# Inverting the scan's unit triangles as 64x64 blocks on the array's diagonal quarters, with a second set of their tiles

## The chip, the cores and the metric

The kernel runs on one core of a Trainium2 chip. Five engines work in parallel, each through its own list of instructions in a fixed order: TensorE (PE in the profile, with PEld for the loading of weights), VectorE (DVE), ScalarE (ACT), GpSimd (POOL) and SyncE (SP), which issues most DMA transfers. They wait for each other through semaphores. The metric is the time of one execution on the device in microseconds; less is better.

## The reference

The program takes 256 tokens of width 1024 through three layers. The change lies in the first one, whose mixer joins dilated window attention (8 heads) with a bidirectional RWKV-7 recurrence (8 heads of 64). Behind it come a PEER feed-forward layer and two layers of another kind. The recurrence, for each head and each of the two directions, is

```python
def wkv7_scan(r, w, k, v, kk, a, reverse):
    def step(state, inp):
        r_t, w_t, k_t, v_t, kk_t, a_t = inp
        sa = jnp.einsum('bhvk,bhk->bhv', state, -kk_t)
        state = (state * w_t[:, :, None, :]
                 + sa[..., :, None] * (kk_t * a_t)[..., None, :]
                 + v_t[..., :, None] * k_t[..., None, :])
        y = jnp.einsum('bhvk,bhk->bhv', state, r_t)
        return state, y
    _, ys = lax.scan(step, state0, xs, reverse=reverse)
```

and the two directions' outputs are added, normalised per head, scaled and gated.

## The kernel before

**Tiling.** The kernel computes the recurrence in chunks of 64 tokens. Inside a chunk the dependence of one step on the earlier ones is a unit triangular 64x64 matrix, which is inverted; between chunks a state is carried. The 8 heads are four pairs `q`, the two heads `i` of a pair on the two halves of the partitions. The 256 tokens are two tiles `t` of 128 tokens, so two chunks each (`HALVES` are the slices 0:64 and 64:128). For each pair there are four inversions, one per direction `d` and tile `t`.

**A pair's steps.** `prepare` (L606 to L679) makes decayed keys and their transposes: its TensorE work is L606, L614, L654, L659 and L670, with chains over VectorE, ScalarE and GpSimd between them (L637, for one, computes the `ar` that L659 transposes). `start(d, t)` multiplies keys with keys (L687) and masks the products to triangles (L691) in the tile PR, which holds for each head a 128x128 matrix with two 64x64 blocks on its diagonal, one per chunk, and zeros elsewhere; the zeros are written once by GpSimd (L591). `tile(d, t)` inverts the triangle by five doubling levels of two half-steps each. In the first half-step two matmuls of 128x128 (L720, one per head) multiply it with X and VectorE masks the result into PP (L721); in the second two matmuls (L725) multiply PP with X, VectorE transposes the result (L727), and a copy makes the new X (L728; `nc.any` leaves the engine to the compiler, mostly ScalarE). L735, L743 and L746 then apply the inverse; `states` (L761, L767, L768, and L595 for the outputs) carries the state over the four chunks; `finish` normalises and gates. An fp32 matmul shows as two records in the trace.

**What sets the order.** The function `weave` gets the generators of all pairs, of the attention heads, of the output projection and of some weights' work, as tasks with a list of tasks that must be done before. Going through the list while the program is built, it takes from the tasks that are free the one whose next piece can begin first by a simple cost estimate, and emits its instructions; each engine's order is then fixed. Before the change `start` of pair q, direction d, tile t waits for the inversion of the same (d, t) of pair q-1, since both use the same PR tile, and X and PP too exist once for each (d, t).

**Lines outside this stage** that the rows show: L1516 and L1523 (two small matmuls of a compressed attention in a later layer; the weights have 64 columns in the one, 64 rows and columns in the other), L1557 (score matmuls of that attention, with weights of 64 rows on either half of the rows), L345 (sums of a weight product, one column), L527, L546 and L552 (attention), L341 (VectorE's part of a weight product), L106 to L108 (weight phases).

## Time and profile before

| | us |
|---|---|
| three runs | 2334.44, 2318.8, 2332.5 |
| median | 2332.5 |
| the profiled execution | 2320.28 |
| its span, first to last instruction | 2318.2 |
| stage of the change, from the first L687 to the next weight phase | 140.3 to 402.2 |

Over the whole span TensorE is busy 2191.8 us (95%), VectorE 1735.9 (75%), ScalarE 1264.6 (55%) and GpSimd 809.6 (35%); the mean granted clock of TensorE is 0.973 of full speed. [...] In the timelines each row is a group of equal instructions one behind another: its start, its length to the end of the last (matmuls are pipelined, so the next group starts before that end), the engine, the line, the operation, output and inputs by the program's names, and the weights' rows by columns, then output partitions by columns. "g", "o" and "y" are tags of PSUM tiles.

### The profile page before, as it was taken

How to read it: one execution, taken by the hardware profiler on the slowest of the kernel's cores; microseconds unless marked ns; L12 is line 12 of the kernel's file. 1: busy time of each engine (PE TensorE's matmuls, PEld its weight loads, DVE VectorE, ACT ScalarE, POOL GpSimd, SP SyncE). 2: the span in 40 equal slices, each digit the busy share in tenths (PEclk: the TensorE clock that was granted, in tenths of full speed). 3: DMA queues.
4: the chain of work that ended last, by engine and by line, in shares of the span. 5: the costliest groups of instructions: out<-in, count | busy, mean ns of one | idle time of the engine just before them, and what ended most of it. 6: DMA issues, size and time to landing. Idle time of an engine off the chain costs nothing.

```text
span 2318.2 us, 46849 instructions
## 1 busy us (share of the span) xinstructions
PE 2191.8 (95%) x17962; PEld 2079.0 (90%) x17962; DVE 1735.9 (75%) x3278; ACT 1264.6 (55%) x2689; POOL 809.6 (35%) x811
## 2 busy tenths in 40 slices
PE   6999898789899999999999999899999999989998
PEld 3878587789799999999999999878899999979998
DVE  6888886899877888777776765678875666777664
ACT  3543532735477776555554644447556666536543
POOL 1132320569877777444444100101432221131000
PEclk8999898899999999999999999999999999989999
DMA  7422123447655666666665675323565555516663
GB/s 266 149 92 86 61 73 96 119 107 173 162 148 155 154 150 177 196 196 195 193 193 165 185 219 193 122 74 111 155 202 166 181 162 191 178 36 192 190 200 119
DMA packets 304064, 358.38 MB, mean 155 GB/s; under 512 B 24188, under 2 KB 276576, under 8 KB 302816
## 3 DMA queue, kind: packets, MB, share of 16 engines
q1 hardware_dynamic: 291456, 349.53, 50.0%
q10 hardware_dynamic: 12384, 5.86, 1.0%
q8 instruction: 141, 2.31, 0.4%
q14 instruction: 83, 0.68, 0.1%
HBM read 354.28 MB, written 1.05 MB: 153 GB/s over the span
## 4 chain that ended last, share of the span: by engine, by line
PE 76%; DVE 13%; DMA 3%; ACT 3%; issue 2%; POOL 2%; SPq 0%; ACTq 0%; DVEq 0%; POOLq 0%
PE g L106 12%; PE g L108 12%; PE g L107 12%; PE o L106 4%; PE o L107 4%; PE o L108 3%; PE g L1162 2%; PE y L1314 2%; PE o L1314 2%; PE y L1312 2%; PE o L1312 2%; PE o L1313 2%; PE y L1313 2%; DVE uT L1001 2%; DVE wl L100 2%
## 5 line engine op out<-in xcount | busy, mean ns | idle before, releaser
L99 ACT ACTIVATE wh<-raw 128x1024 fp32r<-128x1024 f32 (+3 forms) x397 | 387.1, 977 | 389.2 <-PE g L107 185.5
L100 DVE TENSOR_TENSOR wl<-raw,wh 128x1024 fp32r<-128x1024 f32 (+3 forms) x381 | 431.6, 1135 | 223.2 <-ACT wh L99 209.8
L106 PE MATMUL g<-xh,wh 128*128 128x256 f32 x1864 | 529.9, 285 | 8.7 <-ACT xh L374 5.8
L108 PE MATMUL g<-xh,wl 128*128 128x256 f32 x1864 | 525.4, 282 | 8.4 <-DVE wl L100 8.3
L107 PE MATMUL g<-xl,wh 128*128 128x256 f32 x1864 | 524.6, 282 | 4.1 <-DVE xl L375 2.7
L1001 POOL TENSOR_TENSOR ul<-uT,uh 128x512 fp32r<-128x512 f32 x320 | 411.6, 1306 | 188.4 <-ACT uh L1001 188.4
L106 PEld LDWEIGHTS g<-xh,wh 128*128 128x128 f32 x1864 | 357.5, 192 | 15.2 <-ACT xh L374 6.9
L108 PEld LDWEIGHTS g<-xh,wl 128*128 128x128 f32 x1864 | 356.2, 191 | 12.1 <-DVE wl L100 11.7
L107 PEld LDWEIGHTS g<-xl,wh 128*128 128x128 f32 x1864 | 356.4, 191 | 6.1 <-DVE xl L375 3.5
L1001 ACT ACTIVATE uh<-uT 128x512 fp32r<-128x512 f32 x384 | 221.3, 627 | 146.5 <-POOL ul L1001 76.5
L108 PE MATMUL g<-ph,ul 128*128 128x256 f32 x1024 | 291.1, 284 | 7.7 <-POOL ul L1001 7.6
L106 PE MATMUL g<-ph,uh 128*128 128x256 f32 x1024 | 292.8, 286 | 3.7 <-ACT uh L1001 2.0
L107 PE MATMUL g<-pl,uh 128*128 128x256 f32 x1024 | 289.1, 282 | 0.0
L108 PEld LDWEIGHTS g<-ph,ul 128*128 128x128 f32 x1024 | 194.7, 190 | 11.3 <-POOL ul L1001 11.1
L106 PE MATMUL o<-hh,wh 128*128 128x256 f32 x704 | 197.8, 281 | 1.6 <-DVE t L1374 1.6
L106 PEld LDWEIGHTS g<-ph,uh 128*128 128x128 f32 x1024 | 195.1, 191 | 4.6 <-ACT uh L1001 2.3
L107 PE MATMUL o<-hl,wh 128*128 128x256 f32 x704 | 197.4, 280 | 0.0
L108 PE MATMUL o<-hh,wl 128*128 128x256 f32 x704 | 197.1, 280 | 0.0
L107 PEld LDWEIGHTS g<-pl,uh 128*128 128x128 f32 x1024 | 195.3, 191 | 0.0
L1001 DVE TENSOR_TENSOR al<-G,ah 128x256 fp32r<-128x256 f32 x128 | 173.9, 1359 | 17.2
L154 POOL TENSOR_TENSOR sql<-sq,sqh 128x256 fp32r<-128x256 f32 x48 | 48.8, 1018 | 340.1 <-ACT sqh L153 336.0
L1001 DVE STREAM_TRANSPOSE uT<-u 128x1024 f32<-128x1024 f32 x128 | 157.8, 1235 | 2.3 <-DMA u<-in_peer_u_dram 1.9
(772 smaller groups left out, 5456.4 us busy)
## 6 DMA issues: line engine op xcount, KB each, us to landing
u<-in_peer_u_dram SPq DMA_DIRECT2D x512, 128.0 KB, 2.6
raw<-in_ffn_w_gate_dram SPq DMA_DIRECT2D x44, 1024.0 KB, 5.6
raw<-in_ffn_w_up_dram SPq DMA_DIRECT2D x44, 1024.0 KB, 5.3
u<-in_peer_v_dram SPq DMA_DIRECT2D x64, 512.0 KB, 4.3
uT<-in_peer_v_dram SPq DMA_DIRECT2D x64, 512.0 KB, 4.2
raw<-in_ffn_w_down_dram SPq DMA_DIRECT2D x32, 1024.0 KB, 5.1
raw<-in_ada_w_dram SPq DMA_DIRECT2D x24, 1024.0 KB, 5.2
raw<-in_w_in_dram SPq DMA_DIRECT2D x13, 1024.0 KB, 5.7
```

The source lines that it names most:

```text
L99: nc.scalar.activation(h, v, AF.Copy)
L100: self.sub.tensor_tensor(l, v, h.bitcast(F), op=OP.subtract)
L106: nc.tensor.matmul(out, sh, mh, start=first, stop=False)
L107: nc.tensor.matmul(out, sh, ml, start=False, stop=False)
L108: nc.tensor.matmul(out, sl, mh, start=False, stop=last)
L154: self.sub.tensor_tensor(l, sq, h.bitcast(F), op=OP.subtract)
L1001: return lambda *args, **kw: self.tc.keep_in_program_order(f(*args, **kw))
L1162: nc.tensor.matmul(p[:, t], g[:, t], b[:, t], start=True, stop=True)
L1312: nc.tensor.matmul(o, vh[:, s], ah, start=i == 0 and c % 2 == 0, stop=False, skip_group_check=True)
L1313: nc.tensor.matmul(o, vh[:, s], al, start=False, stop=False, skip_group_check=True)
L1314: nc.tensor.matmul(o, vl[:, s], ah, start=False, stop=i == NB - 1, skip_group_check=True)
```

## The change

Every 128x128 block-diagonal matrix of the inversion becomes two 64x64 blocks that lie one above the other, chunk 0 on partitions 0 to 63 and chunk 1 on 64 to 127, so X, PP and the new tile PA (the triangle and the key product that L735 uses) are half as wide. A half-step is four matmuls of 64x64 (head `i`, chunk `r`), each on the quarter of the array that its partitions give, all into one PSUM tile. The masks and the identity are 64 wide. What the outputs still need as a full block-diagonal matrix stays in PR; the finished inverse is copied into a block-diagonal tile TT by two copies, whose zeros GpSimd writes once. PR, PA, X, PP, TT and `sn` get a name that ends in q % 2, so two sets exist. In the list for `weave`, `start` of (q, d, t) now waits for the inversion of (q-2, d, t) instead of (q-1, d, t), and `finish` of q waits for `finish` of q-1.

```diff
@@ -447,23 +447,32 @@
     nc.vector.tensor_tensor(xi, pi, fi, op=OP.bitwise_xor)
     xf = pool.tile([128, 128], F, name="xf")
     nc.vector.tensor_copy(xf, xi)
-    up = pool.tile([128, 128], F, name="up")
-    nc.vector.tensor_tensor(up, pi, fi, op=OP.is_lt)
-    lo = pool.tile([128, 128], F, name="lo")
-    nc.vector.tensor_tensor(lo, pi, fi, op=OP.is_gt)
-    m = keep.tile([128, 2, 8, 128], F, name="masks")
-    t = pool.tile([128, 128], F, name="mt")
+    k.bm = keep.tile([128, 128], F, name="bm")
+    nc.vector.tensor_scalar(k.bm, xf, 64.0, None, op0=OP.is_lt)
+
+    pc = pool.tile([128, 64], I32, name="pc")
+    nc.vector.tensor_scalar(pc, pi[:, 0:64], 63, None, op0=OP.bitwise_and)
+    fc = fi[:, 0:64]
+    xi, xf = xi[:, 0:64], xf[:, 0:64]
+    nc.vector.tensor_tensor(xi, pc, fc, op=OP.bitwise_xor)
+    nc.vector.tensor_copy(xf, xi)
+    up = pool.tile([128, 64], F, name="up")
+    nc.vector.tensor_tensor(up, pc, fc, op=OP.is_lt)
+    lo = pool.tile([128, 64], F, name="lo")
+    nc.vector.tensor_tensor(lo, pc, fc, op=OP.is_gt)
+    m = keep.tile([128, 2, 8, 64], F, name="masks")
+    k.unit = keep.tile([128, 64], F, name="unit")
+    nc.vector.tensor_tensor(k.unit, pc, fc, op=OP.is_equal)
+    t = pool.tile([128, 64], F, name="mt")
     for d, tri in enumerate((up, lo)):
-        nc.vector.scalar_tensor_tensor(m[:, d, 6], xf, 64.0, tri, op0=OP.is_lt, op1=OP.mult)
-        nc.vector.tensor_tensor(m[:, d, 7], m[:, d, 6], k.ident, op=OP.add)
+        nc.vector.tensor_copy(m[:, d, 6], tri)
+        nc.vector.tensor_tensor(m[:, d, 7], tri, k.unit, op=OP.add)
         for i in range(6):
             b = float(1 << i)
             nc.vector.scalar_tensor_tensor(t, xf, b, tri, op0=OP.is_ge, op1=OP.mult)
             nc.vector.scalar_tensor_tensor(m[:, d, i], xf, 2 * b, t, op0=OP.is_lt, op1=OP.mult)
-            nc.vector.tensor_tensor(m[:, d, i], m[:, d, i], k.ident, op=OP.add)
+            nc.vector.tensor_tensor(m[:, d, i], m[:, d, i], k.unit, op=OP.add)
     k.masks = m
-    k.bm = keep.tile([128, 128], F, name="bm")
-    nc.vector.tensor_scalar(k.bm, xf, 64.0, None, op0=OP.is_lt)
 
 
 def selectors(k, pool):
@@ -671,14 +680,16 @@
         self.bon = self.t1("bon")
         nc.vector.tensor_mul(self.bon, self.vT, p)
         self.yp = None
-        self.W, self.PB = [None] * 2, [[None] * 2 for _ in range(2)]
+        self.W, self.PB, self.PA = [None] * 2, [[None] * 2 for _ in range(2)], [[None] * 2 for _ in range(2)]
 
     def start(self, d, t):
 
         k, nc, pool = self.k, self.k.nc, self.late
         up = k.masks[:, d]
         az, btk = self.az[d][:, t].rearrange("p i a t -> p (i a) t"), self.btk[d]
-        PR = self.blocks(pool, f"PR{d}{t}", [128, 2, 2, 2, 128])
+
+        self.PA[d][t] = PA = pool.tile([128, 2, 2, 64], F, name=f"PA{d}{t}{self.q % 2}")
+        PR = self.blocks(pool, f"PR{d}{t}{self.q % 2}", [128, 2, 2, 128])
         self.PB[d][t] = pool.tile([128, 2, 128], F, name=f"PB{d}{t}{self.q % 2}")
         ps = [k.pw([128, 2, 2, 64]) for _ in range(2)]
         for x in range(2):
@@ -687,10 +698,11 @@
                 nc.tensor.matmul(ps[x][r].rearrange("p i a t -> p (i a) t"), btk[:, x, n], az[:, :, r], start=True, stop=True)
         yield
         for x in range(2):
+            nc.vector.tensor_tensor(PA[:, x], ps[x][:, :, 0], up[:, 6, None].to_broadcast([128, 2, 64]), op=OP.mult)
+        for x in range(2):
             for r in HALVES:
-                nc.vector.tensor_tensor(PR[r, :, x, :, r], ps[x][r], up[r, None, 6:8, r].to_broadcast([64, 2, 2, 64]),
-                                        op=OP.mult)
-        nc.gpsimd.tensor_copy(self.PB[d][t], PR[:, :, 0, 1])
+                nc.vector.tensor_tensor(PR[r, x, :, r], ps[x][r, :, 1], up[r, 7, None].to_broadcast([64, 2, 64]), op=OP.mult)
+        nc.gpsimd.tensor_copy(self.PB[d][t], PR[:, 0])
 
     def tile(self, d, t):
 
@@ -699,40 +711,43 @@
             self.yp = k.psum([128, T], tag="y", bufs=2)
         m = k.masks
         up, lo = m[:, d], m[:, 1 - d]
-        bc = lambda x: x[:, None, :].to_broadcast([128, 2, 128])
-        PR = k.zeroed[f"PR{d}{t}"]
-        X = pool.tile([128, 2, 2, 128], F, name=f"X{d}{t}")
-        pp = pool.tile([128, 2, 128], F, name=f"PP{d}{t}")
-        MA = PR[:, :, 0, 0]
-
-        nc.gpsimd.tensor_tensor(MA, MA, bc(k.ident), op=OP.add)
+        bc = lambda x: x[:, None, :].to_broadcast([128, 2, 64])
+        PR, PA = k.zeroed[f"PR{d}{t}{self.q % 2}"], self.PA[d][t]
+        X = pool.tile([128, 2, 2, 64], F, name=f"X{d}{t}{self.q % 2}")
+        pp = pool.tile([128, 2, 64], F, name=f"PP{d}{t}{self.q % 2}")
+        tt = self.blocks(pool, f"TT{d}{t}{self.q % 2}", [128, 2, 128])
+        MA = PA[:, 0]
+
+        ic = [(i, r) for i in range(2) for r in HALVES]
+
+        nc.gpsimd.tensor_tensor(MA, MA, bc(k.unit), op=OP.add)
         nc.gpsimd.tensor_tensor(X[:, 0], MA, bc(up[:, 0]), op=OP.mult)
         yield
 
         nc.vector.transpose(X[:, 1], X[:, 0])
         for i in range(2):
             r = slice(64 * i, 64 * i + 64)
-            self.ymm(i, self.yp[r, t * 128:(t + 1) * 128], self.vn[:, t, r], PR[:, i, 1, 1])
+            self.ymm(i, self.yp[r, t * 128:(t + 1) * 128], self.vn[:, t, r], PR[:, 1, i])
         for lv in range(1, 6):
             yield
-            p = k.pw([128, 2, 128])
-            for i in range(2):
-                nc.tensor.matmul(p[:, i], MA[:, i], X[:, 1, i], start=True, stop=True)
+            p = k.pw([128, 2, 64])
+            for i, r in ic:
+                nc.tensor.matmul(p[r, i], MA[r, i], X[r, 1, i], start=True, stop=True)
             nc.vector.tensor_mul(pp, p, bc(lo[:, lv]))
             yield
-            p = k.pw([128, 2, 128])
-            for i in range(2):
-                nc.tensor.matmul(p[:, i], pp[:, i], X[:, 0, i], start=True, stop=True)
+            p = k.pw([128, 2, 64])
+            for i, r in ic:
+                nc.tensor.matmul(p[r, i], pp[r, i], X[r, 0, i], start=True, stop=True)
             if lv < 5:
                 nc.vector.transpose(X[:, 1], p)
-            nc.any.tensor_copy(X[:, 0], p)
+                nc.any.tensor_copy(X[:, 0], p)
+        for r in HALVES:
+            nc.any.tensor_copy(tt[r, :, r], p[r])
         yield
-        tt = X[:, 0]
-        z0 = pp.rearrange("p i t -> p (i t)")[:, 0:128]
+        z0 = pp.rearrange("p i t -> p (i t)")
         p = k.pw([128, 128])
-        for i in range(2):
-            s = slice(64 * i, 64 * i + 64)
-            nc.tensor.matmul(p[:, s], PR[:, i, 1, 0], self.vn[:, t, s], start=True, stop=True)
+        for i, r in ic:
+            nc.tensor.matmul(p[r, HALVES[i]], PA[r, 1, i], self.vn[r, t, HALVES[i]], start=True, stop=True)
         nc.any.tensor_copy(z0, p)
         yield
         if self.W[d] is None:
@@ -766,7 +781,7 @@
                     p = k.pw([128, 128])
                     nc.tensor.matmul(p, nbk[r, 1, t], self.vn[r, t], start=True, stop=False)
                     nc.tensor.matmul(p, nbk[r, 0, t], u[r], start=False, stop=True)
-                    sn = pool.tile([128, 128], F, name="sn", bufs=6)
+                    sn = pool.tile([128, 128], F, name=f"sn{self.q % 2}", bufs=6)
                     if step:
                         st = pool.tile([128, 128], F, name="st", bufs=2)
                         nc.vector.tensor_add(st, cur[d], p)
@@ -940,10 +955,10 @@
                     first.append((("pre", q), pairs[q].prepare(), tuple(("s", q - 1, d, t) for d in range(2) for t in range(2))
                                   + ((("fin", q - 2),) if q > 1 else ())))
                 first.append((("st", q), pairs[q].states(), tuple((q, d, t) for d in range(2) for t in range(2))))
-                first.append((("fin", q), pairs[q].finish(mix[1][:, q]), (("st", q),)))
+                first.append((("fin", q), pairs[q].finish(mix[1][:, q]), (("st", q),) + ((("fin", q - 1),) if q else ())))
                 for d, t in ((0, 0), (1, 1), (0, 1), (1, 0)):
                     first.append((("s", q, d, t), pairs[q].start(d, t), ((("pre", q),) if q else ())
-                                  + (((q - 1, d, t),) if q else ())))
+                                  + (((q - 2, d, t),) if q > 1 else ())))
                     last.append(((q, d, t), pairs[q].tile(d, t), (("s", q, d, t),)))
             heads = [(("att", h), dilated_attention(k, pt, qk[0], qk[1], vn, mix[0], h), (("att", h - 1),) if h else ())
                      for h in range(8)]
```

In the changed kernel's own numbering the level matmuls are L735 and L740, their VectorE partners L736 and L742 (with the copy L743), the copies into TT L745, the former L735 is L750, `start`'s matmuls L698 and its masks L701 and L704; lines of the second half of the program move by 15.

Each engine's order before and after, at two places. The first is TensorE's list around the `prepare` of pair 1. Names: X00 and PP00 are the tiles of direction 0 and tile 0; az and btk are `start`'s inputs, with the direction behind them; the numbers behind the underscore tell instances apart; "x2" is two matmuls. Before, the starts of pair 1 stand one by one, each behind the last step (L746) of the same tile of pair 0:

```order
L743 MATMUL o128_2003<-PP00_1636,X00_1635 128x64 x2
L725 MATMUL g127_1997<-X11_1639,PP11_1640 128x128 x2
L746 MATMUL o128_2003<-X00_1635,na00_1172 64x128 x2
L687 MATMUL g129_2010<-az0_1122,btk0_1710 64x256 x2
L687 MATMUL g130_2011<-az0_1122,btk0_1710 64x256 x2
L527 MATMUL o131_2017<-qk11_378,qk01_374 128x256 x2
L735 MATMUL g132_2027<-vn0_1063,PR11_1590 128x64 x2
L720 MATMUL g133_2031<-X01_1653,PR01_1600 128x128 x2
```

After the change, with a name's third digit for q % 2, the four starts of pair 1 (inputs btk0_1724 and btk1_1832) stand together right behind the last matmul of its `prepare` (L679), while pair 0's inversions (X000, X110) are still in hand:

```order
L679 MATMUL g102_1916<-kd01_1709,bm_245 128x256
L698 MATMUL o103_1924<-az0_1128,btk0_1724 64x256 x2
L698 MATMUL g104_1925<-az0_1128,btk0_1724 64x256 x2
L345 MATMUL g105_1930<-one_69,acc_1580 128x1 x4
L698 MATMUL g106_1940<-az1_1271,btk1_1832 64x256 x2
L698 MATMUL o107_1941<-az1_1271,btk1_1832 64x256 x2
L698 MATMUL g108_1965<-az0_1128,btk0_1724 64x256 x2
L698 MATMUL g109_1966<-az0_1128,btk0_1724 64x256 x2
L698 MATMUL o110_1982<-az1_1271,btk1_1832 64x256 x2
L698 MATMUL g111_1983<-az1_1271,btk1_1832 64x256 x2
L604 MATMUL y116_2031<-PR001_1921,vn1_1686 64x128 x2
L735 MATMUL g112_1998<-X000_1656,PA000_1587 64x64 x4
```

So the eight groups of L698 moved ahead of pair 0's levels, and pair 1's tiles may begin any time after them.

The second place is TensorE's list while `states` of pair 0 runs (L767, L768 and L595 before; L782 and L783 after) among the inversions of pair 1. L767 and L768 take weights of 64 rows by 128 columns, L720, L725 and L595 here 128 by 128. Before:

```order
L720 MATMUL g168_2253<-X00_2073,PR00_1581 128x128 x2
L725 MATMUL o169_2257<-X11_2077,PP11_2078 128x128 x2
L767 MATMUL g170_2262<-vn0_1063,nbk10_1306 128x128
L768 MATMUL g170_2262<-W10_2041,nbk10_1306 128x128
L720 MATMUL g171_2269<-X01_2132,PR01_1600 128x128 x2
L720 MATMUL o172_2274<-X10_2192,PR10_1620 128x128 x2
L595 MATMUL y75_1634<-ar00_1119,sn_2216 128x64
L725 MATMUL g173_2278<-X00_2073,PP00_2074 128x128 x2
```

After:

```order
L735 MATMUL o157_2345<-X001_2032,PA001_1920 64x64 x4
L740 MATMUL g158_2351<-X111_2038,PP111_2039 64x64 x4
L735 MATMUL g159_2358<-X011_2044,PA011_1961 64x64 x4
L782 MATMUL o160_2368<-vn0_1069,nbk10_1312 128x128
L783 MATMUL o160_2368<-W10_2243,nbk10_1312 128x128
L740 MATMUL g161_2373<-X001_2032,PP001_2033 64x64 x4
L735 MATMUL g162_2380<-X111_2038,PA111_1936 64x64 x4
L555 MATMUL o163_2386<-ident_61,sc_2221 128x128 x4
L740 MATMUL g164_2392<-X011_2044,PP011_2045 64x64 x4
```

Here the inversions of pair 1 (names that end in 1) are groups of 64x64 weights, and between them stand weights of 64 by 128 (L782, L783) and of 128 by 128 (L555).

## Rows read from the trace of the kernel before

**Rows 1.** The head of the page.
```profile
span 2318.2 us, 46849 instructions
```

**Rows 2.** Windows A to F: stretch, length, busy (instructions), granted clock, DMA share, GB/s.
```profile
core 0: us, PE busy (x) PEld busy (x) DVE busy (x) ACT busy (x) POOL busy (x), PEclk, DMA share, GB/s
140.30:169.50 29.20, 25.23 (x163) 18.65 (x163) 27.41 (x72) 13.98 (x35) 15.29 (x21) 0.88 0.07 25
169.50:233.90 64.40, 64.36 (x495) 53.98 (x494) 54.75 (x139) 22.23 (x64) 16.73 (x18) 1.00 0.26 83
233.90:257.60 23.70, 19.58 (x104) 13.89 (x102) 19.08 (x50) 13.74 (x34) 6.41 (x5) 0.78 0.14 46
257.60:279.00 21.40, 18.46 (x133) 12.33 (x134) 20.11 (x51) 5.91 (x14) 12.23 (x14) 1.00 0.18 51
279.00:303.40 24.40, 18.81 (x132) 16.07 (x131) 22.73 (x61) 15.67 (x38) 5.77 (x5) 0.93 0.12 42
303.40:389.80 86.40, 85.46 (x668) 73.59 (x666) 70.79 (x172) 29.06 (x72) 7.77 (x14) 1.00 0.33 105
389.80:402.20 12.40, 6.51 (x26) 4.02 (x26) 4.59 (x11) 2.04 (x5) 0.00 (x0) 0.50 0.20 60
```

**Rows 3.** Waits of TensorE in the stage: total us, times, longest.
```profile
PE o L659 <- DVE ar L637: 6.6, 4, 3.8
```

**Rows 4.** Timeline of TensorE: levels, with two groups of `states` between them; L735.
```profile
187.88 0.56 PE L735 MATMUL o<-vn,PR 128*128 128x64 f32 x4
188.27 1.00 PE L345 MATMUL g<-one,acc 128*128 128x1 f32 x8
...
211.98 0.61 PE L725 MATMUL g<-X,PP 128*128 128x128 f32 x4
212.52 0.49 PE L767 MATMUL g<-vn,nbk 64*128 64x128 f32 x2
212.84 0.38 PE L768 MATMUL g<-W,nbk 64*128 64x128 f32 x2
213.16 0.71 PE L720 MATMUL o<-X,PR 128*128 128x128 f32 x4
213.70 0.61 PE L720 MATMUL g<-X,PR 128*128 128x128 f32 x4
214.15 0.61 PE L725 MATMUL g<-X,PP 128*128 128x128 f32 x4
```

**Rows 5.** Timeline of TensorE: weights of 64 rows or 64 columns, here and later.
```profile
141.62 0.60 PE L687 MATMUL o<-az,btk 128*64 128x256 f32 x4
142.06 0.60 PE L687 MATMUL g<-az,btk 128*64 128x256 f32 x4
...
1497.98 2.05 PE L1516 MATMUL g<-ce,w 128*64 128x30 f32 x32
...
1501.76 0.29 PE L1523 MATMUL o<-cg,w 64*64 64x15 f32 x4
1501.98 0.60 PE L119 MATMUL o<-one,R 1*128 1x1 f32 x4
...
1526.36 0.59 PE L1557 MATMUL g<-kd,qT 64*128 64x256 f32 x2
1526.80 0.27 PE L1556 MATMUL g<-kd,qT 64*128 64x128 f32 x1
...
1527.02 0.38 PE L1557 MATMUL g<-kd,qT 64*128 64x256 f32 x1
1527.13 0.38 PE L1557 MATMUL o<-kd,qT 64*128 64x256 f32 x1
```

**Rows 6.** Groups by form, stage: line, operation, count, busy us, mean ns, idle before.
```profile
L721 DVE TENSOR_TENSOR PP<-g,masks 128x256 f32<-128x256 f32 x52 | 21.2, 413 | 4.2 <-PE g L720 3.5
L727 DVE STREAM_TRANSPOSE X<-g 128x256 f32<-128x256 f32 x41 | 17.4, 433 | 3.3 <-PE g L725 3.2
L763 DVE TENSOR_TENSOR W<-W,g 64x128 f32<-64x128 f32 x15 | 4.2, 283 | 3.4 <-PE g L761 3.1
L591 POOL MEMSET PR<- 128x1024 f32 x3 | 2.8, 947 | 0.0
```

## Prediction

> **What bounds the kernel now.** I read the page's head first: the span is 2318.2 us [rows 1], and the time of that execution is 2320.28 us, 2.1 us more. Everything that the change edits runs in one stage, from the first L687 matmul (140.3 us) to the start of the next weight phase (402.2 us). So I read the windows of that stage next, cut where pair 1's, 2's and 3's `prepare` begin or end on TensorE: A (start of pair 0 and prepare of 1), B (tiles of 0 and 1), C (prepare 2), D, E (prepare 3), F (tiles 2 and 3, to the end) [rows 2]. The reader is to see two kinds of stretch. In B, TensorE is busy 64.36 of 64.40 us, and in the first part of F 85.46 of 86.40, at a granted clock of 1.00: there TensorE alone is the bound. In A, C and E it is busy 25.23 of 29.20, 19.58 of 23.70 and 18.81 of 24.40, while VectorE is busy 27.41, 19.08 and 22.73: there TensorE waits for the chains of `prepare`. The waits say for what: L659, a transpose of `prepare`, waited 6.6 us in four waits for `ar` of VectorE [rows 3]. So an inversion that costs TensorE less is worth its whole saving in B and F, and only a part in A, C and E.

> **TensorE, per instruction.** A half-step of a level (L720 or L725) is two fp32 matmuls of 128x128 weights, which the trace shows as four records. From one such group to the next go 0.45 us (213.70 to 214.15), and 0.39 for L735 (187.88 to 188.27) [rows 4]. There are 160 half-steps (2 directions, 2 tiles, 4 pairs, 5 levels, 2 halves) and 16 L735.

> After the change each is four matmuls of 64x64 weights, eight records. No row of before shows such a group, so I bound it. Records on 64x64 weights occur only at L1523: four, with 15 columns each, take 0.22 us to the next line, a change of weights' shape included [rows 5]. Thirty-two records with 64 columns of weights and 30 moving columns (L1516), one after another, take 2.05 [rows 5], which is 0.064 each, or 0.058 without the drain of the last (about 0.2); so eight in turn would take 0.46 to 0.51. Records on the two row halves of the array do overlap where they alternate: L1557 with 256 moving columns starts 0.11 us apart when its weights stand in the other half than the record before (1527.02 to 1527.13), against 0.44/2 = 0.22 a record when two follow each other in one half (1526.36 to 1526.80) [rows 5]. The new code alternates halves, so eight records should cost four turns, 4 x 0.058 to 4 x 0.064 = 0.23 to 0.26; I take 0.24. The bounds are 0.22 (what L1523's four took) and 0.51.

> [...]

> **Changes of shape.** Where weights of another shape follow, TensorE loses time: from 211.98 to 213.70 are 1.72 us for twelve records with two such changes (128 rows to 64, and back) [rows 4]; twelve at 0.45/4 are 1.35, so a change costs 0.185. I take 0.18 (0.17 to 0.195). Counted along the instruction order of the stage there are 184 such changes before and 283 after, because 64x64 groups now stand between work of 128x128, 128x64 and 64x128. The second piece of the order, shown with the change, is an example: two changes in its eight rows before (into L767 and out of L768), four in its nine rows after (L782, L783, and into and out of L555).

> The sum on TensorE: 160 x (0.45 - 0.24) = 33.6 off, 16 x (0.39 - 0.24) = 2.4 off, 99 x 0.18 = 17.8 on. Net **18.2 us less**. Half of what the smaller blocks save goes into changes of shape.

> **Where it falls.** Groups of levels and L735 together, counted in each stretch of the order, are 17, 68, 3, 8, 22, 58 before in A to F, and 14, 67, 7, 34, 10, 44 after. The changes are 13, 52, 22, 15, 8, 74 and 23, 74, 17, 55, 29, 85. The second set of tiles moves the starts of a pair to just behind its prepare (first piece of the order), so that its levels come earlier: those of pair 2 in D, out of E and F. With these prices, and the other work that changes place (starts, states, attention), TensorE's work changes by about -3, -10, -6, +21, 0, -19 (sum -17.5, within the rounding of 18.2).

> What of it reaches the time? B and F: TensorE has no gap there, but the turn of one tile gets longer than its share of the engine. A half-step's way is 0.24 on TensorE, 0.27 until the last record has drained (0.61 less three starts of 0.11 [rows 4]), 0.28 on VectorE (L763 [rows 6]) and two hand-overs, which no row prices and which I bound by 0.05 and 0.4: together 0.85 to 1.2 us by that estimate; four tiles at 0.24 and their changes fill that barely. Along the new order seven or eight pairs of steps stand closer than that. I charge B 1.8 and F 0.6, hence -8.5 and -18. In C only prepare's own chain is left, so of -6 I count -1; of A's -3, where that chain holds a part, -2; E, -1. In D 21.40 us held 18.46 of TensorE work: of +21 some 3 fall into its gaps, +17.5. The sum is -2 - 8.5 - 1 + 17.5 - 1 - 18 = **-13 us**.

> **VectorE, ScalarE, GpSimd.** L721 took 413 ns on 128x256, L727 433 [rows 6]; at half width they should be near the 283 of L763 (64x128) [rows 6]. 80 x 0.13 plus 80 x 0.14 is 21 us less of VectorE. It is charged at nothing: in B VectorE is busy 54.75 of 64.40, not the bound [rows 2], and with some 70 operations 0.135 shorter it would need 45 to TensorE's 54. The masks of L691, 64 operations, become 96 of half the elements each: charged at nothing, at worst 96 x 0.28 less 64 x 0.28, 9 us, which the 21 cover. The last X now goes to TT by two copies of half the size instead of one: 16 tiles, some 0.3 us later each (one more operation like L763), hidden while three other tiles are in hand. POOL gets 16 memsets instead of 4 (947 ns for 128x1024) [rows 6], in bytes 1.5 times as much, so about 2 us more; it is busy 6.41 of 23.70 in C and so has room. Its two operations at the head of each tile are halved. Weight loads, DMA and `states` are untouched; behind the stage the order of the engines is the same but for one load's place.

> The profiled execution goes from 2320.3 to 2307. The median of before is 12.2 us above that execution, so on the scale of the median: 2332.5 - 13 = **2319**.

> **The rivals.**
> R1, slower: the two halves take turns, by the PSUM tile that they share. The place is each of the 176 groups, the price 0.45 instead of 0.24: +37 on -18.2, so +18.8 (the longer groups cover each other's way, so nothing for stalls): 2351; at 0.50, 2360. The change turns from gain to loss at 0.24 + 13/176 = 0.31. For it: no row shows halves in one tile overlapping. Against: L687's column halves write different partitions of one tile (four records of 256 columns in 0.44, from 141.62 to 142.06) [rows 5], so two may write one tile at once there.
> R2, no gain: each half-step is bound by its way and not by TensorE. If the estimate of 0.85 to 1.2 us is short by 0.08 us for each of the 160 half-steps, 13 us are lost: 2332. For it: B's four tiles alone give the cover. Against: the order has `states`, attention and weights' work in between.
> R3, more gain: A, C and E shrink with VectorE's load, since prepare's operations wait behind half-width ones. Then of TensorE's gaps there, 4.0 + 4.1 + 5.6 us [rows 2], most close: A 24, C 17, E 21 instead of 27, 22.5, 23.4, 11 more, and without the 2.4 of B and F: 2306. For it: VectorE was idle only 2 to 5 us in each. Against: the waits are for long chains over three engines [rows 3].
> [...]

> **How the numbers follow.** The forecast (2312 to 2327 by the bounds of group and change without the turns) has 0.43, R3 0.22, R2 0.17, R1 0.10, R4 0.04; 0.04 remains for a gain beyond R3 (the group at 0.22 and changes at 0.17 too, below 2297). About 1%, 23 us, is what a measurement of this kernel can tell from no change: below 2309 is faster, above 2356 slower. Faster: R3 but for its upper end, and the remainder, 0.25. Slower: R4 and the half of R1 with groups near 0.50, 0.09. Same: 0.66. The range 2297 to 2344 leaves out R1, R4 and the remainder, 0.18.

> **What would show it.** Eight records of the half-steps (L735 and L740 in the changed kernel's own numbering) in 0.22 to 0.26 us would confirm the price; 0.45 or more is R1. The shape changes show as gaps of 0.15 to 0.2 between starts. B should last about 56 us and D 39; C and E about as long as now (R3: 17 and 21). [...] I am wrong most easily in the price of a 64x64 group, which no row shows, and in how the gaps of `prepare` behave when pairs overlap.

## The result, and the profile after

| | median us | lowest to highest | runs |
|---|---|---|---|
| before | 2328.13 | 2316.53 to 2334.44 | 15 |
| changed | 2347.68 | 2334.37 to 2358.59 | 15 |

The changed kernel is slower: its time is 1.0079 of the time before (95% interval 1.0062 to 1.0096), about 19 us, where 13 us less were forecast. Its profiled execution took 2349.32 us, near its median; that of before (2320.28) lies 8 us under the median of its 15 runs, so of the 29 us between the two profiles about 10 are chance. Of the 29 us, 24 lie in the stage, the rest ahead of it and behind it. How far two executions of one stage can lie apart shows the old code with trial stretches behind it (below): in the stage TensorE has the same instructions in the same order, and to the same place, the start of L797, it took 263.7 us instead of 254.1. The two rows, of the kernel before and of that run, have the columns of [rows 2]:

```profile
140.30:394.41 254.11, 235.93 (x1703) 191.24 (x1702) 215.30 (x541) 101.37 (x256) 64.20 (x77) 0.95 0.23 75
140.20:403.88 263.68, 249.11 (x1709) 200.56 (x1707) 215.94 (x543) 101.74 (x256) 63.23 (x78) 0.89 0.23 73
```

TensorE waited less there (14.6 us idle against 18.2), but its clock was lower and its work took 13 us longer.

The windows of the changed kernel, cut at the same places of the program as those of before (A to F, F in two pieces), answer [rows 2]. Columns: stretch, length, busy time (instructions) of the five engines, granted clock, DMA share, GB/s.

```profile
core 0: us, PE busy (x) PEld busy (x) DVE busy (x) ACT busy (x) POOL busy (x), PEclk, DMA share, GB/s
142.70:172.05 29.35, 21.43 (x201) 13.64 (x200) 24.44 (x74) 13.11 (x32) 15.42 (x32) 0.83 0.06 24
172.05:237.08 65.03, 61.27 (x757) 46.67 (x756) 45.36 (x143) 19.96 (x70) 10.51 (x16) 0.84 0.20 66
237.08:261.20 24.12, 15.53 (x104) 10.94 (x104) 19.08 (x50) 14.53 (x35) 5.74 (x5) 0.68 0.26 88
261.20:315.39 54.19, 51.83 (x446) 37.64 (x445) 35.00 (x106) 12.98 (x39) 10.90 (x16) 0.66 0.19 59
315.39:346.00 30.61, 26.95 (x159) 17.65 (x157) 18.47 (x50) 13.50 (x37) 6.05 (x5) 0.61 0.07 19
346.00:416.00 70.00, 68.06 (x724) 54.22 (x724) 53.38 (x155) 20.81 (x54) 5.03 (x12) 0.96 0.33 105
416.00:428.70 12.70, 6.81 (x28) 4.25 (x28) 4.85 (x12) 2.04 (x5) 0.20 (x2) 0.51 0.25 68
```

The stage lasts 286.0 us instead of 261.9. The column to read is the granted clock (PEclk), TensorE's as a share of full speed. Before, it was 1.00 in B, D and the first part of F; now it is 0.84 in B, 0.66 in D and 0.61 in E. Of 54 slices of 1 us of D (261.2 to 315.2) 50 read 0.50 or 1.00, and in the other four, at 0.54 to 0.84, it changes between these two; so a mean of 0.66 says that TensorE spent 68% of D at the lower level, 0.50. Summed over these rows that is 125 us at the lower level, where [rows 2] give 33. (Here and below "low time" is twice the missing share of the clock, times the length. By the mean clock of the whole stage, by which the runs below are compared, it is 126 against 31.)

TensorE's timeline shows what a group costs at either level: the 64x64 groups at 197 us at full clock, those at 205 us at the lower one. Columns as in [rows 4].

```profile
196.87 0.40 PE L735 MATMUL g<-X,PA 64*64 64x64 f32 x8
197.10 0.40 PE L740 MATMUL g<-X,PP 64*64 64x64 f32 x8
197.34 0.40 PE L750 MATMUL o<-vn,PA 64*64 64x64 f32 x8
...
203.57 0.79 PE L782 MATMUL g<-vn,nbk 64*128 64x128 f32 x2
204.16 0.63 PE L783 MATMUL g<-W,nbk 64*128 64x128 f32 x2
204.72 0.69 PE L735 MATMUL o<-X,PA 64*64 64x64 f32 x8
205.20 0.64 PE L740 MATMUL g<-X,PP 64*64 64x64 f32 x8
205.63 0.64 PE L735 MATMUL g<-X,PA 64*64 64x64 f32 x8
```

At full clock a group goes to the next in 0.23 to 0.24 us: the forecast's price, about half of the 0.45 of [rows 4]. At the lower level it takes 0.43 (205.20 to 205.63), so 45% of the time spent there is lost. Eight records in 0.23 us, where eight in turn would take 0.46 or more by the forecast's bound, also mean that the two row halves do overlap in one PSUM tile.

TensorE's waits in the stage (total, times, longest) answer [rows 3], and VectorE's groups [rows 6].

```profile
PE g L668 <- DVE ar L646: 10.0, 3, 4.7
PE y L604 <- DVE PR L704: 3.0, 2, 1.6
PE o L740 <- DVE PP L736: 2.8, 2, 2.5
PE g L740 <- DVE PP L736: 2.0, 3, 1.2
```

```profile
L736 DVE TENSOR_TENSOR PP<-g,masks 128x128 f32<-128x128 f32 x49 | 13.6, 282 | 9.4 <-PE g L735 8.5
L742 DVE STREAM_TRANSPOSE X<-g 128x128 f32<-128x128 f32 x43 | 13.0, 307 | 6.8 <-PE g L740 6.1
```

The half-width VectorE operations take 282 and 307 ns, near the forecast 283. But each engine now waits for the other: L736 waited 8.5 us for L735 where L721 waited 3.5 for L720 (the rows with tag g), and TensorE waits for L736, for the masks (L704) and longer for `prepare` (10.0 us for `ar`, 6.6 before). TensorE is idle 286.0 - 251.9 = 34.1 us of the stage, before 261.9 - 238.4 = 23.5.

### The profile page after: what moved, and what is told of

Same layout as the page of the kernel before. It is cut to its first block, busy times and chain, and to the rows that moved or that the text cites. A ratio compares the mean times of both kernels' runs of the same rounds, so it can differ in the third digit from the quotient of the medians.

```text
span 2347.6 us, 48300 instructions
## 1 busy us (share of the span) xinstructions
PE 2210.6 (94%) x18666; PEld 2074.2 (88%) x18666; DVE 1714.8 (73%) x3319; ACT 1258.7 (54%) x2700; POOL 799.4 (34%) x823
## 4 chain that ended last, share of the span: by engine, by line
PE 74%; DVE 14%; DMA 4%; issue 3%; ACT 3%; POOL 2%; SPq 0%; DVEq 0%; ACTq 0%; POOLq 0%
PE g L106 11%; PE g L108 11%; PE g L107 11%; PE o L106 3%; PE o L107 3%; PE o L108 3%; PE g L1177 2%; PE o L1328 2%; PE y L1328 2%; PE o L1329 2%; PE y L1329 2%; PE y L1327 2%; PE o L1327 2%; DVE uT L1016 2%; DVE wl L100 2%
```

## The experiments

The question was why the clock fell. Theory A1: waits of TensorE bring it down, and the shorter groups made more of them. A2: the 64x64 groups do so themselves, waits or not. B: it is the order with two pairs in hand (two sets of tiles). Each kernel's row of the windows over its whole stage, from the first `start` matmul to the next weight phase, stands in its own part; the columns are those above. Ratios are to the kernel before on the same chip, whose median was 2327.8, 2327.9 and 2328.7 in the three groups of runs; ratio and interval are taken over all runs, so they need not be the quotient of the medians.

**The disputed thing by itself.** Behind the stage of the kernel before stand five trial stretches, each after some 13 us of full 128x128 matmuls (`small` is the four 64x64 matmuls of a half-step, halves in turn; `full` the two 128x128 ones).

```diff
+    for _ in range(150):
+        small(p, B[0])
...
+    for _ in range(45):
+        small(p, B[0])
+        keep(nc.tensor.matmul(w[:, 0, 0:64], e, B[0][:, 0], start=True, stop=True))
...
+    for _ in range(35):
+        full(p, C[0])
+        keep(nc.tensor.matmul(w[:, 0], e[0:64], C[0][0:64, 0], start=True, stop=True))
...
+    for _ in range(35):
+        p = k.psum([128, 2, 64])
+        small(p, B[1])
+        keep(nc.vector.tensor_copy(B[1], p))
...
+    for _ in range(30):
+        p = k.psum([128, 2, 128])
+        full(p, C[1])
+        keep(nc.vector.tensor_copy(C[1], p))
```

> The kernel before with five trial stretches behind the stage, each after 13 us of 128x128 matmuls: (1) 150 groups of four 64x64 matmuls with nothing between them, (2) the same groups, each followed by one matmul of 128x128 weights, so with changes of shape, (3) 128x128 groups alternating with matmuls of 64x128, changes of shape on full blocks, (4) 64x64 groups that each wait for a VectorE copy of the last, (5) 128x128 groups that wait in the same way. Waits alone (A1): 1 to 3 at a clock of 1.00, 4 and 5 fall to 0.50. Blocks alone (A2): 1, 2 and 4 fall, 3 stays, 5 may stay. Changes of shape: 2 and 3 fall, 1 stays. The time is that of before plus about 230 us and says nothing.

The windows of the five, the last two cut where the clock changes, and the timeline of TensorE at these two cuts:

```profile
425.62:460.76 35.14, 35.14 (x1201) 35.07 (x1201) 0.00 (x0) 0.00 (x0) 0.00 (x0) 1.00 0.02 5
473.91:507.26 33.35, 33.35 (x451) 27.33 (x451) 0.00 (x0) 0.00 (x0) 0.00 (x0) 1.00 0.01 2
520.27:557.15 36.88, 36.88 (x212) 28.44 (x210) 0.00 (x0) 0.00 (x0) 0.00 (x0) 1.00 0.00 1
570.30:576.19 5.89, 3.13 (x58) 2.18 (x57) 2.04 (x7) 0.00 (x0) 0.00 (x0) 0.99 0.01 3
576.19:606.15 29.96, 19.34 (x224) 14.15 (x224) 7.88 (x27) 0.00 (x0) 0.00 (x0) 0.50 0.00 1
621.19:627.23 6.04, 3.45 (x22) 2.50 (x20) 2.12 (x5) 0.00 (x0) 0.00 (x0) 1.00 0.00 0
627.23:669.87 42.64, 30.25 (x101) 23.16 (x101) 10.20 (x24) 0.00 (x0) 0.00 (x0) 0.50 0.00 0
```

```profile
575.35 0.45 PE L825 MATMUL g<-bn,ident 64*64 64x64 f32 x8 [0.39 <-DVE bn L849]
576.19 0.69 PE L825 MATMUL g<-bn,ident 64*64 64x64 f32 x8 [0.39 <-DVE bn L849]
577.27 0.69 PE L825 MATMUL g<-bn,ident 64*64 64x64 f32 x8 [0.39 <-DVE bn L849]
578.36 0.69 PE L825 MATMUL g<-bn,ident 64*64 64x64 f32 x8 [0.39 <-DVE bn L849]
...
626.00 0.71 PE L829 MATMUL g<-bc,ident 128*128 128x128 f32 x4 [0.52 <-DVE bc L854]
627.23 1.22 PE L829 MATMUL g<-bc,ident 128*128 128x128 f32 x4 [0.52 <-DVE bc L854]
628.97 1.22 PE L829 MATMUL g<-bc,ident 128*128 128x128 f32 x4 [0.52 <-DVE bc L854]
```

The first three stretches, without a wait, stay at 1.00: 64x64 groups alone (35.14/150 = 0.234 each), the same with changes of shape, and full blocks with changes of shape. The last two, where each group waits for VectorE (0.39 and 0.52 us a time), fall to 0.50 some 6 us after they begin and stay there, whatever the block. So in these stretches waits of a fraction of a microsecond, repeated after every group, bring the clock down by themselves; neither the small block nor the change of shape does. They make up 0.39 of 0.84 us there, far more than in the kernel, where TensorE is idle for 34 of 286 us: the stretches show that waits suffice, not yet that they did it in the kernel. A step of the fourth stretch takes 0.84 us at full clock (575.35 to 576.19) and 1.09 at the lower one (577.27 to 578.36): where TensorE waits anyway, 23% is lost and not 45% (in the fifth 1.23 and 1.74, so 29%). One alternating pair of the second stretch takes 33.35/45 = 0.74; less 0.234 for the group and 0.195 for two records on full weights (half of the 0.39 of L735, [rows 4]), its two changes of shape cost 0.31, an estimate of 0.155 each.

**The blocks alone**: 64x64, but one set of tiles (all six names lose their q % 2) and the old order of starts and `finish`.

```diff
-        X = pool.tile([128, 2, 2, 64], F, name=f"X{d}{t}{self.q % 2}")
+        X = pool.tile([128, 2, 2, 64], F, name=f"X{d}{t}")
...
-                                  + (((q - 2, d, t),) if q > 1 else ())))
+                                  + (((q - 1, d, t),) if q else ())))
```

> The 64x64 blocks with one set of their tiles: names without q % 2, starts wait for the inversion of the pair before again. In the changed kernel TensorE's granted clock stood at its lower level for about 130 us of the stage and its end, before for 48. Theory A (the 64x64 groups bring the clock down): the low time stays above 100 us and the kernel at 2340 to 2350. Theory B (the order with two pairs in hand does, by the waits and changes of shape it makes): low time near 50 us again, 2310 to 2320, faster than before.

```profile
142.00:414.20 272.20, 244.98 (x2413) 179.50 (x2412) 199.43 (x587) 98.20 (x271) 50.99 (x81) 0.82 0.22 70
```

2337.98 us, ratio 1.0030 (1.0004 to 1.0056). The low time is 98 us. The blocks alone bring most of it (theory B falls as the sole cause), but by the medians they explain only half of the loss. (The profiled execution, 2345.77, is one of the slow ones of its ten; the table below has the low time of all.)

**The second set alone**: 128x128 blocks as before, with a second PR, X and PP for two of the four (direction, tile); there is no room in the on-chip memory for all four (the tiles would need 87.25 kB in each partition where 80.16 are left).

```diff
+    def two(self, d, t):
+        return self.q % 2 if d == t else 0
...
-        X = pool.tile([128, 2, 2, 128], F, name=f"X{d}{t}")
+        X = pool.tile([128, 2, 2, 128], F, name=f"X{d}{t}{self.two(d, t)}")
...
-                                  + (((q - 1, d, t),) if q else ())))
+                                  + (((q - 2 + (d != t), d, t),) if q > 1 - (d != t) else ())))
```

> The 128x128 blocks of before, with a second set of PR, X and PP for two of the four (direction, tile), (0,0) and (1,1), whose starts then wait for the pair before the last; there is no room for all four. If the short groups' waits are the cause, full groups with more pairs in hand leave TensorE no more idle than before: low time in the stage 25 to 45 us, time 2320 to 2334. If the order of two pairs itself is the cause (starts in a heap, masks of two pairs on VectorE), waits on the masks and a low time above 60 us, 2338 or more.

```profile
140.50:413.50 273.00, 245.99 (x1708) 195.07 (x1707) 221.87 (x551) 102.48 (x259) 63.10 (x79) 0.92 0.22 70
```

2338.05 us, ratio 1.0036 (1.0014 to 1.0059): the low time (44 us) is what A1 expected, the time what B did. So two of the four second sets cost some 10 us with full blocks too (3 to 14 by the interval). The stage is 11 us longer than before. Idle time grew by 3.5 us (27.0 against 23.5) and low time by 12, at 23 to 45% of itself 3 to 5 us; the rest isn't accounted for, and the profile of before, 8 us under its median, is part of it. With 64x64 blocks it costs the same: 2347.7 against 2338.0. I had not forecast a cost of this part at all.

**Each half-step twice**: the same four matmuls again, into the same place. They were left out of the cost estimate that `weave` uses, yet in the trace TensorE's order still differs from the changed kernel's. So `weave` alone does not fix the order, as the description of the kernel put it; what else does is not shown.

```diff
             for i, r in ic:
                 nc.tensor.matmul(p[r, i], MA[r, i], X[r, 1, i], start=True, stop=True)
+            for i, r in ic:
+                extra(nc.tensor.matmul(p[r, i], MA[r, i], X[r, 1, i], start=True, stop=True))
...
             for i, r in ic:
                 nc.tensor.matmul(p[r, i], pp[r, i], X[r, 0, i], start=True, stop=True)
+            for i, r in ic:
+                extra(nc.tensor.matmul(p[r, i], pp[r, i], X[r, 0, i], start=True, stop=True))
```

> The changed kernel with each half-step's four 64x64 matmuls issued twice into the same place (the result is the same; the order of the instructions differs too, as it is made from estimates). A group then lasts 0.47 us, as long as the 0.45 of before. Theory A1 (the clock falls because shorter groups leave TensorE waiting): the waits are filled, low time back to 50 to 60 us, and the kernel at 2340 to 2352 (the saving of 36 us is given back, the 99 changes of shape at 0.18 remain). Theory A2 (64x64 groups keep the clock low, waits or not): low time 130 us or more, and the doubled groups add 37 us or more: 2385 or above.

```profile
140.10:418.10 278.00, 250.96 (x3692) 198.85 (x3691) 209.52 (x604) 93.74 (x254) 52.86 (x88) 0.91 0.22 69
```

2342.70 us, ratio 1.0060 (1.0034 to 1.0086): 1280 more records on TensorE (37 us of work), and by the medians the kernel is 5 us faster than the changed one (the two intervals overlap, so it is safe to say only that it is no slower). The low time is 50 us. A2 would have had 2385 or more; it falls.

**Only the first half-step twice** (the first of the two additions above).

> As the run with every half-step issued twice, but only the first half-step of each level is doubled: TensorE's work is 18 us less than there (80 groups at 0.235). If the waits decide the clock, the low time lies between that run's (50 us in the stage) and the changed kernel's (126). If it stays near 60, the kernel comes to 2325 to 2332, no slower than before; if it goes back above 100, the gain is given away again and it stays at 2340 to 2350.

```profile
140.20:416.80 276.60, 246.93 (x3052) 188.81 (x3051) 205.49 (x594) 95.69 (x264) 55.10 (x88) 0.86 0.22 70
```

2333.97 us, ratio 1.0040 (1.0019 to 1.0060), low time 77 us: between the two, as A1 has it; a little above the 2325 to 2332 of its better branch.

**Idle matmuls in `prepare`**, ten per direction, on values that come ready while TensorE waits for `ar`; in the kernel before and in the changed one. Their results are unused.

```diff
+    def fill(self, x, n=2):
+        p = self.k.psum([128, T])
+        for _ in range(n):
+            extra(self.k.nc.tensor.matmul(p, x[:, 0:128], x, start=True, stop=True))
...
             self.kd.append(kd)
+            self.q and self.fill(kd)
...
             nc.scalar.activation(ep, L, AF.Exp)
+            self.q and self.fill(ep)
```

> The kernel before, with idle matmuls in prepare of pairs 1 to 3: ten of 128x256 for each direction, on values that come ready one after another while TensorE waits for ar (about 4.3 us of TensorE each time, 26 in all, results unused). If waits bring the clock down, the low time of the stage falls from 31 us to under 15, which gives back about 8; the idle matmuls cost what they exceed the 13 us of waits, 5 to 15. So 2320 to 2337. If waits don't matter, the low time stays at about 30 and the time is 2338 to 2350.

> The changed kernel with the same idle matmuls in prepare. If the low clock begins at the waits of prepare, the low time of the stage falls from 126 us to 60 to 90, worth 18 to 33 us, less 5 to 15 that the idle matmuls exceed the waits by: 2325 to 2342. If the short waits inside the inversion decide it, the low time stays above 100 and the time is 2350 to 2370.

First the kernel before with them, then the changed one:

```profile
140.20:428.60 288.40, 264.56 (x1829) 214.48 (x1828) 227.06 (x559) 101.38 (x251) 61.17 (x77) 0.96 0.21 66
```

```profile
141.60:429.10 287.50, 256.70 (x2533) 195.68 (x2532) 203.85 (x593) 95.50 (x265) 54.21 (x88) 0.88 0.21 67
```

2353.17 us (1.0116, 1.0082 to 1.0151) and 2354.63 us (1.0111, 1.0069 to 1.0153). As a remedy both failed, and my sums for them were 12 to 16 us too low: the idle matmuls fill few waits. What they tell is the clock: in the changed kernel the low time fell from 126 to 69 us though no half-step was touched. That it begins at the waits of `prepare` is not shown by this, for TensorE's idle time fell by only 3 us (34.1 to 30.8); the added 128x256 matmuls may do it as dense work. In the kernel before it fell from 31 to 23, not under 15, and that is less than the old code varies by itself (25 and 58 us in its two rows shown with the result).

**One set of tiles, with the first half-step, or both, issued twice.**

> 64x64 blocks with one set of tiles, and the first half-step of each level issued twice. If the two parts add up as they did so far (the second set cost the 64x64 kernel 10 us, 2348 against 2338; doubling the first half-step gave back 14, 2348 to 2334), this is 2324 (2318 to 2331), level with the kernel before or just under it, with a low time of 40 to 75 us in the stage. If instead the low clock in the one-set kernel has another cause than short groups, doubling only adds its 18 us of work: 2345 to 2356.

> 64x64 blocks with one set of tiles, and both half-steps issued twice, so that a group is as long as before (0.47 against 0.45). What then remains of the change is VectorE's shorter work (21 us, charged at nothing) and some 110 more changes of shape, at 0.155 to 0.19 us: 17 to 21 us more on TensorE. If short groups bring the clock down: a low time in the stage of 25 to 45 us as before, and 2333 to 2348 from the changes of shape alone. If the low time stays near 98, the blocks themselves and not their shortness do it.

```profile
140.50:408.90 268.40, 244.10 (x3052) 186.13 (x3051) 202.65 (x592) 96.37 (x266) 50.95 (x80) 0.87 0.22 72
```

```profile
141.40:415.70 274.30, 252.97 (x3693) 199.02 (x3692) 204.84 (x597) 96.27 (x261) 49.59 (x80) 0.91 0.22 71
```

The first came to 2323.96 us, ratio 0.9977 (0.9960 to 0.9994), low time 70 us: the sum of the parts (2324) to the microsecond, which is luck in part, as the interval leaves 4 us to either side. It is the only kernel here that is faster than before, by 4.7 us. (Its profiled execution, 2329.42, is its slowest run; its windows are to be read with that.) The second came to 2334.24, ratio 1.0027 (1.0010 to 1.0044), as expected from the changes of shape; its low time, 49 us, is a little above the 25 to 45. With doubled half-steps the second set costs 10.0 us (2333.97 against 2323.96) and 8.5 us (2342.70 against 2334.24), as it did without.

**All kernels side by side.** Every run's mean clock over the whole program is on record too, so the low time can be had for all runs and not for the profiled one alone. It includes the rest of the program, where nothing changed.

| | idle of TensorE in the stage, us | low time in the stage, us | low time of the whole run, median, us | runs |
|---|---|---|---|---|
| before | 23.5 | 31 | 140 | 58 |
| changed | 34.1 | 126 | 216 | 15 |
| one set | 27.2 | 98 | 198 | 10 |
| full blocks, second set | 27.0 | 44 | 138 | 8 |
| first half-step twice | 29.7 | 77 | 159 | 10 |
| both twice | 27.0 | 50 | 126 | 9 |
| one set, first half-step twice | 24.3 | 70 | 144 | 12 |
| one set, both twice | 21.3 | 49 | 135 | 12 |
| before, idle matmuls | 23.8 | 23 | 120 | 4 |
| changed, idle matmuls | 30.8 | 69 | 169 | 4 |

The clock goes with the time where no instruction differs: over the 15 runs of the changed kernel (182 to 236 us of low time) a straight line rises by 0.37 us for each us of low time, over the 58 of before (111 to 168) by 0.21. Making both half-steps longer again takes the low time back to that of before (126 and 135 against 140), with the same 64x64 blocks: it was the shortness of the groups that lowered the clock. But TensorE's idle time does not put the kernels in order: at 27 us of it the low time in the stage is 98, 44 and 50. So the link between short groups and the low clock is not the sum of the waits that the trace shows, and which of them, or what beside them, makes it is open.

## Why the prediction was wrong

**The prices were right.** A 64x64 group at full clock takes 0.234, forecast 0.24. R1 is out: groups that take turns would need 0.46 or more, and the trace gives half of that; two matmuls on diagonal quarters that write different partitions of one tile overlap. A half-step's way was put at 0.85 to 1.2 us with hand-overs that no row priced; a step of the fourth trial stretch, whose group also waits for VectorE and VectorE for it, took 0.84 at full clock. There are 283 changes of shape, as counted, and by the second trial stretch one costs some 0.155, forecast 0.18. VectorE's half-width operations are nearly as short as assumed.

**The step that failed is "What of it reaches the time?".** It charged each wait with its own length, 5 us in all, put the clock at nothing in the sum, and left a fall of it over all of B, R4, a chance of 0.04. [Rows 2] held the warning: in every stretch where TensorE waited (A, C, E and the stage's end) the clock was below 1.00, and where it did not (B and F's first part) at 1.00; only D, idle for 2.9 us, kept 1.00. I read the low clock as part of `prepare`, not as something that other stretches could get, although I had written that four tiles of shorter groups "fill that barely". Together they were a reason to give the clock more than 0.04. What the profile shows instead: in the stage TensorE's busy time is 13.5 us longer (251.9 against 238.4) where the sum had 18.2 less, and its idle time 10.6 longer where 5 were charged. Of the 37 us between forecast and profiled stage some 32 are slower work and 5 the waits themselves.

The clock accounts for this by stretches, within wide bounds. Low time costs 23% (where TensorE waits) to 45% (where it doesn't) of itself; in A, C, E and F I count only the low time beyond that of [rows 2]. Taken off what was measured:

| | low time counted | measured | less the clock's cost | forecast |
|---|---|---|---|---|
| A | 3 | 29.4 | 28.0 to 28.7 | 27.2 |
| B | 21 | 65.0 | 55.6 to 60.2 | 56 |
| C | 5 | 24.1 | 21.9 to 23.0 | 22.5 |
| D | 37 | 54.2 | 37.6 to 45.7 | 39 |
| E | 20 | 30.6 | 21.4 to 25.9 | 23.4 |
| F | 6 | 82.7 | 80.0 to 81.3 | 80.8 |

Each forecast lies in or within a microsecond of its bounds, which are up to 8 us wide. The stage was forecast 13 us shorter and is 24 us longer; the 92 us of added low time cost 21 to 41, and that difference is 37. By the medians of all runs the added low time is 76 us; at 0.21 to 0.37 of itself that is an estimate of 16 to 28 us out of the 33 between forecast and measurement. So the clock is most of the miss or half of it, not surely all.

**The rivals.** R4 named the mechanism, the clock at its lower level where short groups leave TensorE waiting, but put it in B alone and as all or nothing, for 54 us; it came as low time in D, B and E, for 21 to 41. R2 named the place (a half-step's way), which may be part of what starts it: TensorE waited 4.8 us for L736. But all of its idle time grew by 10.6 us, where R2 needed 13 beside the 5 I had charged, and waits of that length alone would not have reached 2348. R3 is out: A and C are no shorter, E is longer.

**The second set** was costed at nothing beyond its changes of shape. Undoing it is worth 8.5 to 10 us in three pairs of kernels by the medians (8 to 15 by the ratios), and adding it to full blocks costs 10 too. Much of it is waiting: TensorE's idle time in the stage is 5 to 7 us longer with the second set in the three pairs and 3.5 in the fourth, while the low time of the whole run is 15 to 18 us longer in two of the four and no longer in the others. Which wait it is, is not settled: TensorE waits for the masks of the starts that now stand together (3.0 us for L704), but no run took that wait away.

**What stays open** is also by what the short groups lowered the clock: idle matmuls in `prepare` removed 57 us of low time, longer half-steps 49 to 76, and these overlap; in none of these did idle time fall by more than some 7 us.

## What to carry to other kernels

Before work is taken off an engine that is the bound, ask what will fill its place: on TensorE the clock can fall (in D from 1.00 to 0.66), and at the lower level, 0.50, a 64x64 group takes 0.43 us, nearly the 0.45 of the full block at full clock, so the whole saving is gone there. Read the granted clock of every stretch beside the waits, and of every run beside its time: stretches with waits and a clock below 1.00 (here A, C and E, 0.78 to 0.93) next to gapless ones at 1.00 (B) are the sign that there is something to lose. And of a change in two parts, test each alone: here the part meant to give cover (the second set) cost 10 us with either block size, while the smaller blocks were worth 5 us once the first half-steps were made longer again (with both made longer they cost 6).

## What was not expected of the hardware

```profile
286.00:293.00 7.00, 6.54 (x74) 4.84 (x72) 3.00 (x11) 2.24 (x8) 2.50 (x2) 0.96 0.47 150
294.00:317.00 23.00, 23.00 (x172) 15.89 (x168) 12.21 (x32) 7.24 (x20) 0.00 (x0) 0.50 0.18 55
```

For 23 us the records show no gap, and the clock remained at 0.50; in the 7 us ahead of the fall TensorE had stood still for only 0.46 us. The kernel with one set of tiles shows the same in B: 0.34 us of waiting in 10.24, then 13.7 us without a gap at the lower level.

```profile
187.73:197.97 10.24, 9.90 (x117) 7.30 (x114) 7.30 (x23) 4.33 (x15) 6.77 (x11) 1.00 0.29 90
197.97:211.63 13.66, 13.66 (x91) 9.04 (x90) 8.70 (x28) 1.46 (x5) 2.38 (x5) 0.50 0.13 38
```

Between the fourth and the fifth trial stretch, by contrast, full 128x128 matmuls brought the clock back while they ran:

```profile
606.15:610.00 3.85, 3.85 (x11) 3.13 (x10) 0.29 (x1) 0.00 (x0) 0.00 (x0) 0.50 0.02 4
610.00:621.19 11.19, 11.19 (x53) 9.78 (x53) 0.00 (x0) 0.00 (x0) 0.00 (x0) 0.99 0.00 0
```

What raises it in the mixture of D, and what let it fall there after so short a wait, no run here shows. These stretches hold much of the added low time (21 of the 37 us in D), so "waits lower the clock" is shown for the trial stretches and only argued for the kernel.
